# Dense expert stage: half of the PSUM sums leave through ScalarE, and gates lie in runs of 32 tokens

## The chip, the cores and the metric

The kernel runs on one core of one Trainium2 chip. The metric is device time in microseconds (us), the median of several runs; before the change it is 3537.24 us over 3 runs (3536.96 to 3545.42).

The core's engines are named as the profile names them: PE is TensorE's matmul stream and PEld its weight loads, DVE is VectorE, ACT is ScalarE, POOL is GpSimd, SP is SyncE. Each runs its own list of instructions in order. Matmuls write to PSUM, which has eight banks of 128 partitions by 512 float32.

## The reference

One decoder block over 1024 tokens of width 1024. First come RWKV-7 time mixing and differential attention, merged by gates. The change touches what follows, a feed-forward layer of 16384 single-vector experts. Each token picks 16 experts in each of 8 heads; an expert is a pair of keys (e1, e2), each one of 128:

```
ids   = e1 * 128 + e2                        # 8 x 16 experts per token
gates = softmax(vals)                        # per head
act   = gelu(sum_d u_tab[ids] * h) * gates   # 128 numbers per token
y     = sum_e act[e] * v_tab[ids[e]]
x     = x + y                                # then the final RMSNorm
```

## The kernel before

**Two ways through the experts.** For the first four blocks of 128 tokens, `peer` gathers the chosen rows of the tables: POOL issues an indirect DMA (L792) that brings one row of 1024 for each of 128 tokens into a tile `uv`, of which there are five. DVE forms the dot product with `hb` (L814) or adds the row, weighted, to `acc` (L821). That is 512 gathers from `u` and 512 from `v`. For the last four blocks (512 tokens) `dense` computes all 16384 experts and multiplies by a gate that is zero where the token did not choose the expert.

**The gates stage.** `gates` builds the dense gates, four tokens at a time. DVE makes one-hot tiles of the first key (`oh`, L833) and of the second (`ohb`, L837); ACT scales the second by the gate values (`ohg`, L842); PE multiplies the two for each token into a bank `gb` (L843): 128 second keys on the partitions by 128 first keys. ACT copies `gb` into `st` (L844), and every 32 tokens a DMA writes `st` to the scratch tensor `gd_s`, in groups of CE = 4 first keys. PE takes each float32 product as two MATMUL instructions, so 512 products are 1024 of them. Meanwhile `ahead` computes the first 16 values of `ua` below and keeps them in `a_s`.

**The dense stage.** `dense` loops over the 128 first keys e. `head(e)` loads two half tiles of `u` (`wraw`), splits each into a high and a low part (ACT `whi` L153, DVE `wlo` L154), multiplies them with the normalized tokens into a PSUM bank `ua`, takes GELU on ACT (`gw`, L883), multiplies by the gates on DVE (L884), and splits the product (ACT `ah` L175, DVE `al` L176) and two half tiles of `v` (`vh` L175, `vl` L176). The gates of four keys come in one tile `gt` of [512 tokens, 4 keys], so that L884 reads every fourth element of it.

The outputs are eight tiles (four token blocks by two halves of 512 columns). Six stay in PSUM banks `yk` through all 128 keys. The other two ("moved") have no bank of their own: for every second e, `rest` sums CV = 2 keys into a bank `yr`, and DVE adds that bank to `acc` in SBUF (L904), 128 times in all. `yr` and `ua` share the two banks of `zbank`.

**What sets the order.** The code is written as one program, and a tile scheduler places the instructions on each engine at build time, by its own costs. It sets the operations of `peer`, which come last in the program, between those of the gates stage and of the dense stage. From then on each engine's list is fixed.

Of the kernel before, what the change touches and what calls it, by code (L numbers as in the profile page):

```python
# [8 lines left out]
F32 = mybir.dt.float32  # L9
# [4 lines left out]
AF = mybir.ActivationFunctionType  # L14
OP = mybir.AluOpType
# [3 lines left out]
P = 128  # L19
# [17 lines left out]
NE = 16  # L37
# [2 lines left out]
CHO = (1, 1, 1, 1, 0)  # L40
CHB = CH * (CH + 1)
CE = 4
CV = 2
NV = (8, 6)

# [2 lines left out]
def body(ctx: ExitStack, tc: tile.TileContext, ins, out, dbg=None):  # L48
    nc = tc.nc
# [9 lines left out]
    def zbank(name):  # L59
        return ps.tile([P, 512], F32, name=name, tag="zb", bufs=2)  # L60
# [4 lines left out]
    def abank(name):  # L65
        return ps.tile([P, 512], F32, name=name, tag="ab", bufs=2)
# [10 lines left out]
    def at(name, dt=F32):  # L77
        return hp.tile([P, 512], dt, name=name, tag="at", bufs=NA)
# [4 lines left out]
    def t4(name):  # L83
        return hp.tile([P, D], F32, name=name, tag="t4", bufs=N4)
# [89 lines left out]
    def split(src, hi, lo):  # L174
        nc.scalar.activation(hi, src, AF.Copy)  # L175
        nc.vector.tensor_tensor(lo, src, hi.bitcast(F32), op=OP.subtract)  # L176

    def mm3(o, ah, al, bh, bl, first, last):
        nc.tensor.matmul(o, ah, bh, start=first, stop=False)  # L179
        nc.tensor.matmul(o, ah, bl, start=False, stop=False)  # L180
        nc.tensor.matmul(o, al, bh, start=False, stop=last)  # L181
# [614 lines left out]
    def finish(acc, rows, pool, tag, bufs):  # L796

        ssq = pool.tile([P, 1], F32, name="ssqf", bufs=2)
        fnw = pool.tile([P, D], F32, name="fnw", tag=tag, bufs=bufs)
        nc.scalar.activation(fnw, acc, AF.Square, accum_out=ssq)  # L800
        nc.sync.dma_start(fnw, ins["fnw"].to_broadcast([P, D]))
        r = invroot(ssq, 1, 1.0 / D, 1e-6, pool=pool)
        nc.vector.scalar_tensor_tensor(acc, acc, r[:, 0:1], fnw, op0=OP.mult, op1=OP.mult)
        nc.sync.dma_start(out[rows, :], acc)
# [19 lines left out]
    def gates(sp, a, sl, eye8):  # L824

        e1, g = sl[:, 0:P], sl[:, 2 * P:3 * P]
        e2 = sl[:, 3 * P:].bitcast(BF)[:, 0:P]
        nc.scalar.activation(e2, sl[:, P:2 * P], AF.Copy)
        for q in range(0, P, 32):
            st = sp.tile([P, P // CE, 32, CE], F32, name="st", bufs=2)  # L830
            for t in range(0, 32, 4):
                o1 = sp.tile([P, 4, P], F32, name="oh", bufs=4)
                nc.vector.tensor_tensor(o1, eye_row[:, None, :].to_broadcast([P, 4, P]),  # L833
                                        e1[:, q + t:q + t + 4, None].to_broadcast([P, 4, P]), op=OP.is_equal)
                if t % 8 == 0:
                    o2 = sp.tile([P, P, 8], BF, name="ohb", bufs=2)
                    nc.vector.tensor_tensor(o2, eye8, e2[:, None, q + t:q + t + 8].to_broadcast([P, P, 8]),  # L837
                                            op=OP.is_equal)
                b = abank("gb")
                o3 = sp.tile([P, 4, P], F32, name="ohg", bufs=2)  # L840
                for k in range(4):
                    nc.scalar.activation(o3[:, k], o2[:, :, t % 8 + k], AF.Copy, scale=g[:, q + t + k:q + t + k + 1])  # L842
                    nc.tensor.matmul(b[:, k * P:(k + 1) * P], o3[:, k], o1[:, k], start=True, stop=True)  # L843
                nc.scalar.activation(st[:, :, t:t + 4, :].rearrange("p c t f -> p t c f"),  # L844
                                     b.rearrange("p (t c f) -> p t c f", t=4, f=CE), AF.Copy)
            s0 = a * P + q
            nc.sync.dma_start(ins["gd_s"][:, :, s0:s0 + 32, :].rearrange("c p t f -> p c t f"), st)

    def dots(e, W, fh, fl):
        b = zbank("ua")[:, :W]  # L850
        wmul(b, ins["ut"][e], lambda k: fh[:, k, :W], lambda k: fl[:, k, :W], step=8)
        return b
# [8 lines left out]
    def dense(t0, W, fh, fl):  # L861

        TT = W // P
        fp = ctx.enter_context(tc.tile_pool(name="fp", bufs=1))
        acc = []
        for a in range(TT):
            acc.append(t4("accd"))
            nc.sync.dma_start(acc[a], ins["x1s"][t0 + a * P:t0 + (a + 1) * P, :])
        outs = [(a, 0) for a in range(TT)] + [(a, 1) for a in range(TT)][::-1]
        banks = (rbank, rbank, rbank, obank, abank, abank)  # L870
        kept = {o: f("yk") for o, f in zip(outs, banks)}
        moved = outs[len(banks):]
        gt = [None]

        def head(e):

            if e % CE == 0:
                gt[0] = fp.tile([P, 512, CE], F32, name="gt", bufs=2)
                nc.sync.dma_start(gt[0][:, :W], ins["gd_s"][e // CE, :, 0:W, :])
            w = fp.tile([P, 512], F32, name="gw", bufs=2)[:, :W]  # L880
            if e < NE:
                nc.sync.dma_start(w, ins["a_s"][e, :, 0:W])
            nc.scalar.activation(w, w if e < NE else dots(e, W, fh, fl), AF.Gelu)  # L883
            nc.vector.tensor_tensor(w, w, gt[0][:, :W, e % CE], op=OP.mult)  # L884
            v = []
            ah, al = at("ah", F32R)[:, :W], at("al", F32R)[:, :W]
            split(w, ah, al)
            for h, c in enumerate(HALVES):
                raw = fp.tile([P, 512], F32, name="vraw", bufs=NVR)
                nc.sync.dma_start(raw, ins["v"][e * P:(e + 1) * P, c])  # L890
                v.append([fp.tile([P, 512], F32R, name=n, tag=f"v{h}", bufs=NV[h]) for n in ("vh", "vl")])
                split(raw, *v[h])
            return ah, al, v

        def add(o, b, r, first, last):
            ts = slice(o[0] * P, (o[0] + 1) * P)
            mm3(b, r[0][:, ts], r[1][:, ts], *r[2][o[1]], first, last)

        def rest(o, rs):
            b = zbank("yr")  # L900
            for i, r in enumerate(rs):
                add(o, b, r, i == 0, i == CV - 1)
            y = acc[o[0]][:, HALVES[1]]
            nc.vector.tensor_tensor(y, y, b, op=OP.add)  # L904

        rs = [head(0)]
        for e in range(P):
            nxt = head(e + 1) if e + 1 < P else None
            full = rs[:CV] if e % CV == 0 and e else None
            if full:  # L910
                rs = rs[CV:]
            for n, (o, b) in enumerate(kept.items()):
                if full and n in MV:
                    rest(moved[MV.index(n)], full)
                add(o, b, rs[-1], e == 0, e == P - 1)
            rs.append(nxt)
        for o in moved:
            rest(o, rs[:CV])
        for a in range(TT):
            for h in range(2):  # L920
                if (a, h) in kept:
                    y = acc[a][:, HALVES[h]]
                    nc.vector.tensor_tensor(y, y, kept[a, h], op=OP.add)
            finish(acc[a], slice(t0 + a * P, t0 + (a + 1) * P), fp, "gt", 2)
# [13 lines left out]
    if "nopeer" not in dbg:  # L938
        with tc.tile_pool(name="sp", bufs=1) as sp:
            eye_f = sp.tile([P, P * 8], F32, name="eye_f", bufs=1)  # L940
            nc.sync.dma_start(eye_f, ins["eye8"])
            eye8 = sp.tile([P, P, 8], BF, name="eye8", bufs=1)
            nc.vector.tensor_copy(eye8.rearrange("p e t -> p (e t)"), eye_f)
            o = W - ND * P
            fh, fl = fh[:, :, o:W], fl[:, :, o:W]
            for a, c in enumerate(late[o // P:]):
                gates(sp, a, choose(*c), eye8)
                ahead(sp, ND * P, fh, fl, range(a * NE // ND, (a + 1) * NE // ND))
            todo += [(c[2], *choose(*c)) for c in late[:o // P]]
        dense(t0 + o, ND * P, fh, fl)  # L950
        for t in todo:
            peer(*t)


def prepare(inputs):
# [31 lines left out]
    for b in (16, 32):  # L987
# [17 lines left out]

SCRATCH = {"x1s": (T, D), "hfs": (T, D), "k_s": (4, P, T), "v_s": (4, P, T),
           "y_s": (4, 8, P, 512), "g_s": (4, 16, P, 512),
           "gd_s": (P // CE, P, 512, CE), "a_s": (NE, P, 512),
           "m_s": (2, 2, 8 * CHB), "z_s": (2, 2, 8 * CHB)}


# [16 lines left out]
```

## Time and profile before

| | us |
|---|---|
| median of 3 runs | 3537.24 |
| the profiled execution | 3524.41 |
| its span, first to last instruction | 3522.5 |
| PE / DVE / ACT / POOL busy | 3075.7 / 2923.6 / 1363.1 / 1332.3 |

The profile is of one execution, 0.4% below the median of the runs. Times count from the start of its span. The gates stage lies about 1637 to 1967, the dense stage (first to last L904) 2033 to 3483, and the end of `peer` and the final norms 3483 to 3523. A row of a group gives its busy time, the mean duration of one in ns, and the idle time of its engine just before them with what ended that time. Successive instructions of DVE overlap a little, so busy time is below count times mean.

### The profile page before, as it was taken

The numbers are of one execution on the slowest core, as the hardware profiler recorded it, in microseconds if no ns is written. First come the engines' busy times: TensorE is split into PE (matmuls) and PEld (weight loads), VectorE is DVE, ScalarE is ACT, GpSimd is POOL, SyncE is SP. The second block draws the span as 40 slices with busy tenths as digits, with TensorE's granted clock in tenths as the row PEclk, the third lists the DMA queues.
The fourth block names the chain that finished last, engine by engine and source line by source line (L and its number), as shares of the span: only waits on it lengthen the run. The fifth ranks groups of instructions, "written<-read, shape, count | busy, mean of one in ns | idle before, by whom it ended". The sixth has DMA issues, their size and how long they took to land. (4 is left out here: it accounts for less than half of the span.)

```text
span 3522.5 us, 50906 instructions
## 1 busy us (share of the span) xinstructions
PE 3075.7 (87%) x17382; PEld 2399.4 (68%) x17382; DVE 2923.6 (83%) x6546; ACT 1363.1 (39%) x2506; POOL 1332.3 (38%) x1036
## 2 busy tenths in 40 slices
PE   6999998998778966798888589999999999899994
PEld 5777776776556654676666467777777777777773
DVE  4656558978888878999877689998999999899998
ACT  3444434443424421336989433222223232222321
POOL 0000000025543454411223336655655655556554
PEclk9999999989788987899988799999999999999997
DMA  4222444257675789854678989999999999999997
GB/s 129 76 75 72 121 162 155 83 165 239 217 255 178 253 293 311 289 183 136 208 215 279 323 314 342 353 349 341 348 343 351 348 350 354 348 344 357 340 336 270
DMA packets 407524, 898.68 MB, mean 255 GB/s; under 512 B 69024, under 2 KB 140000, under 8 KB 403168
## 3 DMA queue, kind: packets, MB, share of 16 engines
q0 software_dynamic: 147456, 536.94, 43.7%
q1 hardware_dynamic: 259808, 358.49, 30.2%
q8 instruction: 137, 2.24, 0.3%
q14 instruction: 123, 1.01, 0.1%
HBM read 829.22 MB, written 66.07 MB: 254 GB/s over the span
## 5 line engine op out<-in xcount | busy, mean ns | idle before, releaser
L792 POOL DMA_INDIRECT uv<-u,ids x512 | 663.8, 1296 | 1259.3 <-DVE uv L814 622.4
L792 POOL DMA_INDIRECT uv<-v,ids x512 | 667.4, 1304 | 534.3 <-DVE acc L821 379.8
L821 DVE SCALAR_TENSOR_TENSOR acc<-uv,act,acc 128x1024 f32<-128x1024 f32 x512 | 655.5, 1280 | 63.8 <-DMA uv<-v,ids 57.2
L814 DVE SCALAR_TENSOR_TENSOR uv<-uv,hb 128x1024 f32<-128x1024 f32 x512 | 615.6, 1218 | 74.1 <-DMA uv<-u,ids 73.5
L153 ACT ACTIVATE whi<-wraw 128x512 fp32r<-128x512 f32 x552 | 344.2, 629 | 702.2 <-PE z L169 205.5
L168 PE MATMUL ua<-fh,whi 128*128 128x512 f32 x1024 | 427.8, 418 | 95.2 <-DVE accd L904 71.8
L154 DVE TENSOR_TENSOR wlo<-wraw,whi 128x512 fp32r<-128x512 f32 x552 | 373.3, 684 | 140.4 <-ACT whi L153 129.8
L169 PE MATMUL ua<-fl,whi 128*128 128x512 f32 x1024 | 421.5, 412 | 0.0
L175 ACT ACTIVATE ah<-gw 128x512 fp32r<-128x512 f32 x128 | 80.8, 631 | 657.2 <-DVE gw L884 657.2
L179 PE MATMUL yk<-vh,ah 128*128 128x512 f32 x768 | 305.3, 398 | 21.8 <-DMA gw<-a_s 18.1
L168 PEld LDWEIGHTS ua<-fh,whi 128*128 128x128 f32 x1024 | 203.6, 199 | 160.8 <-DVE accd L904 91.8
L180 PE MATMUL yk<-vl,ah 128*128 128x512 f32 x768 | 305.2, 397 | 7.6 <-DVE vl L176 7.5
L181 PE MATMUL yk<-vh,al 128*128 128x512 f32 x768 | 304.9, 397 | 1.3 <-DVE al L176 1.3
L168 PE MATMUL z<-hh,whi 128*128 128x512 f32 x672 | 275.5, 411 | 1.0 <-ACT whi L153 1.0
L172 PE MATMUL z<-hh,wlo 128*128 128x512 f32 x672 | 274.5, 409 | 0.6 <-DVE wlo L154 0.6
L169 PE MATMUL z<-hl,whi 128*128 128x512 f32 x672 | 274.6, 409 | 0.0
L172 PE MATMUL ua<-fh,wlo 128*128 128x512 f32 x1024 | 264.7, 399 | 6.2 <-DVE wlo L154 6.2
L843 PE MATMUL gb<-oh,ohg 128*128 128x128 f32 x1024 | 227.5, 343 | 42.4 <-ACT ohg L842 41.9
L843 PEld LDWEIGHTS gb<-oh,ohg 128*128 128x128 f32 x1024 | 167.0, 210 | 105.7 <-ACT ohg L842 69.3
L169 PEld LDWEIGHTS ua<-fl,whi 128*128 128x128 f32 x1024 | 203.8, 199 | 43.7
L842 ACT ACTIVATE ohg<-ohb,sl 128x128 f32<-128x128 bf16 x512 | 230.1, 551 | 1.9 <-DVE ohb L837 1.9
L172 PEld LDWEIGHTS ua<-fh,wlo 128*128 128x128 f32 x1024 | 195.0, 191 | 49.9 <-DVE wlo L154 7.1
(320 smaller groups left out, 5672.3 us busy)
## 6 DMA issues: line engine op xcount, KB each, us to landing
wraw<-ut SPq DMA_DIRECT2D x256, 256.0 KB, 6.3
vraw<-v SPq DMA_DIRECT2D x256, 256.0 KB, 6.6
wraw<-w_in SPq DMA_DIRECT2D x168, 256.0 KB, 2.8
gd_s<-st SPq DMA_DIRECT2D x16, 2048.0 KB, 12.4
gt<-gd_s SPq DMA_DIRECT2D x32, 1024.0 KB, 9.2
wraw<-wq SPq DMA_DIRECT2D x64, 256.0 KB, 2.8
g_s<-sgo SPq DMA_DIRECT2D x32, 256.0 KB, 2.7
wraw<-proj SPq DMA_DIRECT2D x32, 256.0 KB, 4.2
```

The costliest lines, as they stand in the source:

```text
L153: nc.scalar.activation(hi, raw, AF.Copy)
L154: nc.vector.tensor_tensor(lo, raw, hi.bitcast(F32), op=OP.subtract)
L168: nc.tensor.matmul(o, hi, xh(k), start=(k == 0), stop=False)
L169: nc.tensor.matmul(o, hi, xl(k), start=False, stop=False)
L172: nc.tensor.matmul(o, lo, xh(k), start=False, stop=(k == n - 1))
L179: nc.tensor.matmul(o, ah, bh, start=first, stop=False)
L180: nc.tensor.matmul(o, ah, bl, start=False, stop=False)
L181: nc.tensor.matmul(o, al, bh, start=False, stop=last)
L792: nc.gpsimd.indirect_dma_start(out=t, out_offset=None, in_=ins[src], in_offset=bass.IndirectOffsetOnAxis(ap=ids[:, j:j + 1], axis=0))
L814: nc.vector.scalar_tensor_tensor(u, u, 1.0, hb, op0=OP.mult, op1=OP.mult, accum_out=act[:, j:j + 1])
L821: nc.vector.scalar_tensor_tensor(acc, v, act[:, j:j + 1], acc, op0=OP.mult, op1=OP.add)
L843: nc.tensor.matmul(b[:, k * P:(k + 1) * P], o3[:, k], o1[:, k], start=True, stop=True)
```

## The change

Three edits. First, in `gates` the four products of a bank are interleaved: token k of four takes every fourth column from k on, so that ACT's copy writes, for each first key, four tokens that lie side by side. `st`, `gd_s` and `gt` then hold, for each first key, QT = 32 contiguous tokens. Second, L884 reads `gt` in runs of 32 contiguous elements. Third, `rest` copies `yr` to a new SBUF tile `ye` (two of them) by ACT, and DVE adds `ye`.

```
-            st = sp.tile([P, P // CE, 32, CE], F32, name="st", bufs=2)
+            st = sp.tile([P, P, QT], F32, name="st", bufs=2)
...
-                    nc.tensor.matmul(b[:, k * P:(k + 1) * P], o3[:, k], o1[:, k], start=True, stop=True)
-                nc.scalar.activation(st[:, :, t:t + 4, :].rearrange("p c t f -> p t c f"),
-                                     b.rearrange("p (t c f) -> p t c f", t=4, f=CE), AF.Copy)
-            s0 = a * P + q
-            nc.sync.dma_start(ins["gd_s"][:, :, s0:s0 + 32, :].rearrange("c p t f -> p c t f"), st)
+                    nc.tensor.matmul(b[:, k:512:4], o3[:, k], o1[:, k], start=True, stop=True)
+                nc.scalar.activation(st[:, :, t:t + 4], b.rearrange("p (e t) -> p e t", t=4), AF.Copy)
+            nc.sync.dma_start(ins["gd_s"][:, :, (a * P + q) // QT].rearrange("c p f t -> p c (f t)"),
+                              st.rearrange("p (c f) t -> p c (f t)", f=CE))
...
-                gt[0] = fp.tile([P, 512, CE], F32, name="gt", bufs=2)
-                nc.sync.dma_start(gt[0][:, :W], ins["gd_s"][e // CE, :, 0:W, :])
+                gt[0] = fp.tile([P, 512 // QT, CE, QT], F32, name="gt", bufs=2)
+                nc.sync.dma_start(gt[0][:, :W // QT], ins["gd_s"][e // CE, :, 0:W // QT])
...
-            nc.vector.tensor_tensor(w, w, gt[0][:, :W, e % CE], op=OP.mult)
+            w3 = w.rearrange("p (q t) -> p q t", t=QT)
+            nc.vector.tensor_tensor(w3, w3, gt[0][:, :W // QT, e % CE, :], op=OP.mult)
...
+            t = fp.tile([P, 512], F32, name="ye", bufs=2)
+            nc.scalar.activation(t, b, AF.Copy)
             y = acc[o[0]][:, HALVES[1]]
-            nc.vector.tensor_tensor(y, y, b, op=OP.add)
+            nc.vector.tensor_tensor(y, y, t, op=OP.add)
```

The lists of PE and POOL keep their order. Below the lists are given as they stand; line numbers after the change are larger by one to three (L884 becomes L885, L904 becomes L907, L175 becomes L176, L821 becomes L822).

ACT in the dense stage, the stretch of one key e in which `rest` runs, before and then after:

```order
L883 ACTIVATE gw<-ua 128x512
L175 ACTIVATE ah<-gw 128x512
L175 ACTIVATE vh<-vraw 128x512 x3
L153 ACTIVATE whi<-wraw 128x512 x2
L883 ACTIVATE gw<-ua 128x512
```

```order
L883 ACTIVATE gw<-ua 128x512
L905 ACTIVATE ye<-yr 128x512
L176 ACTIVATE ah<-gw 128x512
L176 ACTIVATE vh<-vraw 128x512
L905 ACTIVATE ye<-yr 128x512
L176 ACTIVATE vh<-vraw 128x512 x2
L154 ACTIVATE whi<-wraw 128x512 x2
L883 ACTIVATE gw<-ua 128x512
```

Where nothing stood between the split of `gw` and those of `v`, there are now two copies of `yr`: one ahead of `ah` (in some places behind it), and one ahead of the second and third `vh` and of `whi`.

DVE at the end of the dense stage, from the last `vl` on, before and then after:

```order
L176 TENSOR_TENSOR vl<-vraw,vh 128x512
L904 TENSOR_TENSOR accd<-accd,yr 128x512
L821 SCALAR_TENSOR_TENSOR acc<-uv,act,acc 128x1024
L923 TENSOR_TENSOR accd<-accd,yk 128x512 x4
L821 SCALAR_TENSOR_TENSOR acc<-uv,act,acc 128x1024
L923 TENSOR_TENSOR accd<-accd,yk 128x512 x2
L904 TENSOR_TENSOR accd<-accd,yr 128x512
L821 SCALAR_TENSOR_TENSOR acc<-uv,act,acc 128x1024
L904 TENSOR_TENSOR accd<-accd,yr 128x512
```

```order
L177 TENSOR_TENSOR vl<-vraw,vh 128x512
L907 TENSOR_TENSOR accd<-accd,ye 128x512
L822 SCALAR_TENSOR_TENSOR acc<-uv,act,acc 128x1024
L926 TENSOR_TENSOR accd<-accd,yk 128x512
L822 SCALAR_TENSOR_TENSOR acc<-uv,act,acc 128x1024
L926 TENSOR_TENSOR accd<-accd,yk 128x512 x5
L822 SCALAR_TENSOR_TENSOR acc<-uv,act,acc 128x1024
L907 TENSOR_TENSOR accd<-accd,ye 128x512 x2
```

Behind the last of these rows the list before still holds 13 operations on gathered rows (L821), and the list after 3 (L822). From the first L884 on there are 658 such operations (L814 and L821) in either list; ten of them have moved from behind the last L904 to places among the 128 keys.

## Rows read from the trace of the kernel before

**Rows 1.** Stages: busy time and count of each engine, granted clock, DMA share, GB/s

```profile
core 0: us, PE busy (x) PEld busy (x) DVE busy (x) ACT busy (x) POOL busy (x), PEclk, DMA share, GB/s
1637.00:1967.00 330.00, 279.34 (x1245) 206.60 (x1244) 270.56 (x642) 305.39 (x684) 80.52 (x67) 0.90 0.73 224
...
2033.00:3483.00 1450.00, 1362.41 (x5702) 1085.27 (x5700) 1346.57 (x1796) 417.92 (x723) 836.26 (x641) 0.98 0.95 343
3483.00:3523.00 40.00, 0.00 (x0) 0.00 (x0) 27.91 (x84) 5.64 (x10) 10.97 (x9) 0.50 0.73 256
```

**Rows 2.** Waits in the dense stage: us in total, times, longest us

```profile
ACT ah L175 <- DVE gw L884: 653.3, 118, 9.8
POOL uv L792 <- DVE acc L821: 264.1, 156, 7.2
...
PE ua L168 <- DVE accd L904: 71.8, 39, 5.4
...
DVE uv L814 <- DMA uv<-u,ids: 48.7, 63, 2.3
```

**Rows 3.** Waits of DVE alone in the dense stage, rest of the list

```profile
DVE acc L821 <- DMA uv<-v,ids: 32.4, 55, 2.2
DVE gw L884 <- ACT gw L883: 12.0, 7, 4.2
```

**Rows 4.** Groups of DVE's and ACT's instructions, 2000 to 3522

```profile
L154 DVE TENSOR_TENSOR wlo<-wraw,whi 128x512 fp32r<-128x512 f32 x221 | 147.3, 684 | 0.0
...
L884 DVE TENSOR_TENSOR gw<-gw,gt 128x512 f32<-128x512 f32 x128 | 138.1, 1079 | 13.0 <-ACT gw L883 13.0
...
L904 DVE TENSOR_TENSOR accd<-accd,yr 128x512 f32<-128x512 f32 x128 | 86.7, 678 | 0.0
...
L883 ACT ACTIVATE gw<-ua 128x512 f32<-128x512 f32 x112 | 67.0, 598 | 118.3 <-PE ua L172 118.2
```

**Rows 5.** One line: a product whose second operand has runs of 64 (L306)

```profile
L306 DVE TENSOR_TENSOR KR<-kk,Ep x8: 679/686/691, 93.9 to 1222.7; 128x512 f32<-128x512 f32 x8
```

**Rows 6.** Gathered tiles in the dense stage: count, ns min/median/max; issue to landing

```profile
L792 POOL DMA_INDIRECT uv<-v,ids x375: 932/1145/1947, 2075.9 to 3480.1; - x188
L821 DVE SCALAR_TENSOR_TENSOR acc<-uv,act,acc x371: 1266/1284/1331, 2092.8 to 3481.6; 128x1024 f32<-128x1024 f32 x186
L814 DVE SCALAR_TENSOR_TENSOR uv<-uv,hb x271: 1207/1218/1295, 2031.9 to 3227.9; 128x1024 f32<-128x1024 f32 x136
...
DMA to landing us min/median/max: 4.5/7.2/11.7
```

**Rows 7.** Stretches of 50 us with the highest DMA share, columns as rows 1

```profile
2483.00:2533.00 50.00, 47.15 (x192) 37.72 (x192) 45.90 (x77) 13.94 (x24) 30.23 (x24) 0.93 0.98 359
2633.00:2683.00 50.00, 44.74 (x182) 35.78 (x181) 45.69 (x70) 13.26 (x24) 26.93 (x22) 0.93 0.98 368
2933.00:2983.00 50.00, 48.52 (x207) 38.40 (x206) 46.91 (x79) 14.76 (x26) 27.69 (x22) 1.00 0.98 359
3183.00:3233.00 50.00, 44.81 (x186) 35.56 (x185) 47.81 (x79) 14.24 (x25) 31.76 (x24) 0.97 0.99 369
```

**Rows 8.** PE in the gates stage, in order of time: start, us

```profile
1722.69 1.54 PE L172 MATMUL ua<-fh,wlo 128*128 128x512 f32 x6
...
1725.27 1.59 PE L843 MATMUL gb<-oh,ohg 128*128 128x128 f32 x8
```

**Rows 9.** Group of the gate products, gates stage

```profile
L843 PE MATMUL gb<-oh,ohg 128*128 128x128 f32 x1024 | 227.5, 343 | 42.4 <-ACT ohg L842 41.9
```

**Rows 10.** ScalarE lines L842 and L828: 128 elements, strided and contiguous

```profile
L842 ACT ACTIVATE ohg<-ohb,sl x512: 502/523/682, 1643.5 to 1963.6; 128x128 f32<-128x128 bf16 x171
...
L828 ACT ACTIVATE sl<-sl x4: 300/302/310, 1642.0 to 1892.7; 128x128 bf16<-128x128 f32 x4
```

**Rows 11.** The last L904, and the last operation on a gathered row

```profile
3482.76 0.68 DVE L904 TENSOR_TENSOR accd<-accd,yr 128x512 f32<-128x512 f32 x1
...
3505.02 1.28 DVE L821 SCALAR_TENSOR_TENSOR acc<-uv,act,acc 128x1024 f32<-128x1024 f32 x1
```

More of the change, by code (lines that the diff above doesn't have):

```diff
@@ L42 @@
 CE = 4
+QT = 32
 CV = 2
@@ L828, in gates @@
         nc.scalar.activation(e2, sl[:, P:2 * P], AF.Copy)
-        for q in range(0, P, 32):
-            st = sp.tile([P, P // CE, 32, CE], F32, name="st", bufs=2)
-            for t in range(0, 32, 4):
+        for q in range(0, P, QT):
+            st = sp.tile([P, P, QT], F32, name="st", bufs=2)
+            for t in range(0, QT, 4):
                 o1 = sp.tile([P, 4, P], F32, name="oh", bufs=4)
@@ L1007 @@
            "y_s": (4, 8, P, 512), "g_s": (4, 16, P, 512),
-           "gd_s": (P // CE, P, 512, CE), "a_s": (NE, P, 512),
+           "gd_s": (P // CE, P, 512 // QT, CE, QT), "a_s": (NE, P, 512),
            "m_s": (2, 2, 8 * CHB), "z_s": (2, 2, 8 * CHB)}
```

## The prediction

> **What bounds the kernel now.** I read first where the three edits act, in the busy time by stages [rows 1], since the shares over the whole span are means over stages with different limits. One edit acts in the gates stage (1637 to 1967), the other two in the dense stage (2033 to 3483). In the dense stage three resources look full at once: PE is busy for 1362.4 of 1450 us, DVE for 1346.6, and the DMA engines for 0.95 of the time at 343 GB/s. ACT has 417.9 us of work there and POOL 836.3. So the second thing to read is who waits for whom. DVE waits for nothing that PE makes: its waits are for gathered rows, 48.7 us at L814 and 32.4 us at L821, and 12.0 us for ACT [rows 2, 3]. Its row L904 has no idle time before it [rows 4], so PE has always finished `yr` when DVE comes to it. The others wait for DVE: ACT 653.3 us for the product with the gates (L884), POOL 264.1 us for L821 to free a buffer, PE 71.8 us for L904 to free a bank [rows 2]. DVE, in its fixed order, is therefore what sets the pace of the dense stage; the gathers are close behind it, and PE has little room.
>
> In the gates stage ACT is busy for 305.4 of 330 us, and PE waits 41.9 us for its `ohg` [rows 1, 9]: ACT bounds it.
>
> **The change part by part.** Step 1, L884 with contiguous gates. The row has 128 instructions of 1079 ns [rows 4]. The same operation on two contiguous tiles takes 684 ns (L154) [rows 4], and with a second operand in runs of 64 it takes 686 ns (L306) [rows 5], so runs of 32 should cost nothing. That is 128 x (1079 - 684) = 50.6 us off DVE, in its own order, with ACT's `ah` waiting right behind it. Bounds: a run of 32 could cost twice the little that a run of 64 does, which leaves 50 us; at worst the product keeps its 1079 ns, and the saving is zero.
>
> Step 2, the add from SBUF. L904 reads a bank and takes 678 ns; with both operands in SBUF I take L154's 684 [rows 4]: 128 x 6 ns = +0.8 us. So moving the operand makes the add no shorter here.
>
> [...]
>
> Step 3, the copy of `yr`. ACT gains 128 instructions like L883, which reads a bank of the same size in 598 ns [rows 4]: 76.5 us. ACT goes from 417.9 to about 494 of 1450 us, so this lies beside other work. It is a new wait in ACT's order: behind a copy stand `ah`, or two `vh` and `whi`, for which DVE and then PE wait. I cost that at nothing: DVE comes to the first add after the product with the gates, and as a rule after `al` as well, so that PE has long finished `yr`, and ACT has hundreds of us of waiting to put the copy in. If the cover were gone, each add would wait for one ACT copy, 128 x 0.6 = 77 us; that is the upper bound. Below nothing: PE's 71.8 us of waiting for L904 go, since the bank is free about 0.6 us after PE fills it. I count no gain, because DVE does not wait for PE. PE's next wait is for DVE's splits.
>
> Step 4, the gate products. The 1024 PE instructions now write every fourth column. No row of before shows a strided PSUM write. Eight of these instructions take 1.59 us [rows 8], so a column leaves about every 1.59 / 8 / 128 = 1.55 ns; six of `ua` take 1.54 us with 512 columns each, one column every 0.50 ns. The write could be three times slower than a contiguous one before it showed, so I take zero. From above: strided reads did cost, L884's 1079 against 684, a factor of 1.58, and ACT's 523 against 302 ns [rows 10]. A factor of 1.58 on 199 ns is 1024 x 0.115 = 118 us, of which PE's idle time in the stage, 330 - 279.3 = 50.7 us, takes up part: 67 us later. No mechanism gives a gain here. ACT's copy into `st` writes runs of four elements before and after, and the DMAs keep size and destination.
>
> [...]
>
> Step 5, ten gathered operations moved from the end into the dense stage. DVE's work from 2033 to the end stays the same: ten of about 1.2 us more before the last add, ten fewer behind it. I therefore make the sum over both stretches.
>
> Step 6, what is late next. DVE's work from 2033 to the end of the span (3522.5) is 1346.6 + 27.9 = 1374.5 us [rows 1], and its idle time 1489.5 - 1374.5 = 115. With 50 us less work the gathers have to come faster. Five buffers go round: POOL's instruction (1.15), the way to landing (7.2) and the operation itself (1.28) are 9.6 us, 1.9 us for each of five [rows 6]; 371 + 271 = 642 operations in 1450 us are one every 2.26 us. So the present pace has some room, but landings of up to 11.7 us already make DVE wait. From one side the extra waits are zero or a little below, since shorter stretches without L821 make smoother demand. From the other, the gathers keep their pace and take back all 50 us. Which is nearer: the four stretches of 50 us in which the DMA engines were busiest, 0.98 to 0.99 at 359 to 369 GB/s [rows 7], have DVE busy for 45.90, 45.69, 46.91 and 47.81, mean 46.6, against a mean of 1346.6 / 29 = 46.4 over the dense stage. More traffic than the change needs (343 x 1450 / 1415 = 351 GB/s) came without more waiting. I take 15 us, on the side of these rows.
>
> Sum: -50.6 + 0.8 + 15 = -34.8 us. The profiled execution took 3524.4 us, its span and 1.9 around it; 3489.6 after it, a factor of 0.990. On the median shown, 3537.2, that is 3502 us.
>
> **Rivals.** (a) The strided write slows the gate products. For it: both strided reads in SBUF are slow. Against it: these products hand over columns at a third of the rate of `ua`. Place: L843, in the gates stage. With the factor above the stage ends 67 us later, net +32, 3569 us. It decides the sign once the stage grows by more than 35 us, that is when an instruction takes (50.7 + 35) / 1024 = 0.084 us more than its 0.199.
>
> (b) The gathers set the pace. For it: 0.95 DMA share, and DVE's 81.1 us of waits on them. Against it: the busiest stretches [rows 7], and POOL's waits for DVE. The dense stage then keeps its length, and only the end, where DVE runs on from the last L904 at 3482.76 to the last L821 at 3505.02 [rows 11], gets shorter, some 0 to 10 us: 3527 to 3537.
>
> (c) ACT's order delays the splits: a copy that waits for PE holds up `vh` and `whi`. For it: ACT's list is fixed. Against it: L904 had no idle time before it. At 77 us of waits less the 35 gained it is +42, 3579 us.
>
> (d) The gates' layout does not shorten L884, because something other than the stride makes it slow. Against it: L306. Time as before, 3537 us.
>
> (e) The whole saving and more: gathers no later, PE freed of its 71.8 us, DVE's idle time shorter by some 15. That is -65 us, 3472.
>
> **How the numbers follow.** A difference of 0.3%, 10.6 us, is about what a measurement of this kernel can tell from none. The forecast, 3475 to 3523 around 3502, has a chance of 0.66; (a) 0.10, (b) 0.13, (c) 0.04, (d) 0.03, (e) 0.04. Faster than 3526.6: the forecast and (e), 0.70. Within 0.3%: (b) and (d), 0.16. Slower: (a) and (c), 0.14. The range goes from 3470, just below (e), to 3540, above (b) and (d); it leaves out the two slower rivals and a little below.
>
> **What would show it.** L885 near 684 ns, and `ye` copies near 600 ns on ACT. No wait of PE for the add of `yr`. L907 without idle time before it; if it has some, with ACT as its releaser, step 3 was wrong. PE's gate products at 1.6 us for eight and the gates stage still 330 us long; if not, step 4. DVE's waits for gathers in the dense stage 80 to 100 us; if they are at 130, the pace was the gathers' and step 6 was wrong. The end from the last add to the end of the span about half of its 40 us. A time above 3527 would make the prediction wrong.

## The result and the profile after

The changed kernel takes 3514.4 us (median of 6 runs, 3502.6 to 3524.1) against 3540.4 of the kernel before in the same comparison: ratio 0.9927, 95% interval 0.9907 to 0.9946, that is 26 us or 0.7% faster. The forecast was 35 us.

The two profiled executions differ less, 3524.4 and 3514.0 us. The stretch up to the gates stage, whose instructions stand in the same order in both kernels, took 1640 us before and 1656 after; in the later runs it lay between 1633 and 1666. So I compare from the gates stage on. From the first one-hot tile to the first add of `yr` it is 393.3 us before and 388.0 after, from there to the last such add 1449.1 and 1446.0, and from there to the end 39.7 and 22.1. The first of these three stretches tells nothing of the change: in the later runs it took 387.8 to 389.3 us with the gates as before and 387.4 to 392.1 with the new ones.

The stages of the kernel after (start and end, length, busy time of PE, PEld, DVE, ACT and POOL, then clock, DMA share, GB/s); the second row begins with the first add and answers to the dense row of [rows 1]:

```profile
1655.00:1979.00 324.00, 275.45 (x1229) 204.27 (x1228) 267.01 (x629) 304.04 (x682) 80.17 (x66) 0.89 0.73 226
...
2044.10:3490.80 1446.70, 1363.65 (x5705) 1082.92 (x5703) 1311.99 (x1805) 467.33 (x850) 851.31 (x650) 0.98 0.95 347
3490.80:3512.20 21.40, 0.00 (x0) 0.00 (x0) 15.74 (x73) 5.63 (x10) 0.00 (x0) 0.50 0.67 245
```

DVE has 34 us less work in the dense stage, although ten more gathered operations lie in it, and yet the stage is only 3 us shorter. What became of the rest stands in the waits there (us in total, times, longest):

```profile
ACT ah L176 <- DVE gw L885: 720.4, 112, 11.6
...
DVE uv L815 <- DMA uv<-u,ids: 63.1, 72, 3.5
DVE acc L822 <- DMA uv<-v,ids: 48.2, 71, 2.1
...
PE ua L169 <- ACT ye L905: 39.9, 12, 5.9
...
ACT ye L905 <- PE yr L182: 30.6, 32, 7.3
```

DVE's waits for gathered rows rose from 81.1 us [rows 2, 3] to 111.3. The groups that answer to [rows 4]:

```profile
L155 DVE TENSOR_TENSOR wlo<-wraw,whi 128x512 fp32r<-128x512 f32 x225 | 150.9, 688 | 9.8 <-ACT whi L154 9.6 <-PE ua L173 0.2
L885 DVE TENSOR_TENSOR gw<-gw,gt 128x512 f32<-128x512 f32 x128 | 88.4, 691 | 17.0 <-ACT gw L883 17.0
L907 DVE TENSOR_TENSOR accd<-accd,ye 128x512 f32<-128x512 f32 x128 | 87.8, 686 | 0.0
```

The product with the gates (L885) fell from 1079 to 691 ns; the add (L907) went from 678 to 686.

### The profile page after: what moved, and what is told of

Read it like the earlier page. It is cut to its first block, busy times and chain, and to the rows that moved or that the text cites. A ratio compares the mean times of both kernels' runs of the same rounds, so it can differ in the third digit from the quotient of the medians.

```text
span 3512.2 us, 51039 instructions
## 1 busy us (share of the span) xinstructions
PE 3085.0 (88%) x17382; PEld 2404.1 (68%) x17382; DVE 2876.8 (82%) x6546; ACT 1412.5 (40%) x2634; POOL 1334.3 (38%) x1036
## 5 line engine op out<-in xcount | busy, mean ns | idle before, releaser
L793 POOL DMA_INDIRECT uv<-u,ids x512 | 655.2, 1280 | 1255.3 <-DVE uv L815 626.6
L793 POOL DMA_INDIRECT uv<-v,ids x512 | 677.9, 1324 | 519.2 <-DVE acc L822 372.4
L822 DVE SCALAR_TENSOR_TENSOR acc<-uv,act,acc 128x1024 f32<-128x1024 f32 x512 | 655.4, 1280 | 72.2 <-DMA uv<-v,ids 65.7
L169 PE MATMUL ua<-fh,whi 128*128 128x512 f32 x1024 | 419.7, 410 | 61.5 <-ACT ye L905 39.9
L176 ACT ACTIVATE ah<-gw 128x512 fp32r<-128x512 f32 x128 | 80.8, 632 | 727.0 <-DVE gw L885 723.1
L844 PE MATMUL gb<-oh,ohg 128*128 128x128 f32 x1024 | 228.3, 344 | 40.3 <-ACT ohg L843 37.8
```

The source lines that it names most:

```text
L169: nc.tensor.matmul(o, hi, xh(k), start=(k == 0), stop=False)
L793: nc.gpsimd.indirect_dma_start(out=t, out_offset=None, in_=ins[src], in_offset=bass.IndirectOffsetOnAxis(ap=ids[:, j:j + 1], axis=0))
L822: nc.vector.scalar_tensor_tensor(acc, v, act[:, j:j + 1], acc, op0=OP.mult, op1=OP.add)
L844: nc.tensor.matmul(b[:, k:512:4], o3[:, k], o1[:, k], start=True, stop=True)
```

## The experiments

All ratios are to the kernel before on the same chip. The columns in us are from one profiled execution each: from the first add of `yr` to the last, from there to the end, and DVE's waits for gathered rows between the two adds. The runs come from several chips: the kernel before took 3516.6 us on that of e1 to e4, 3543.0 on that of e5 to e8, 3513.3 on that of f1 and f2. So the ratios are the safer comparison between these groups. NVR is the number of tiles into which `v` is loaded ahead, 6 where nothing is said.

| kernel | buffers | ratio (95%) | dense | end | waits |
|---|---|---|---|---|---|
| before | 5 | 1 | 1449.1 | 39.7 | 81.1 |
| whole change | 5 | 0.9927 (0.9907 to 0.9946) | 1446.0 | 22.1 | 111.3 |
| e1 layout only | 5 | 0.9934 (0.9916 to 0.9953) | 1433.6 | 39.8 | 104.8 |
| e2 copy only | 5 | 0.9963 (0.9951 to 0.9976) | 1463.1 | 21.5 | 87.6 |
| e4 before | 6 | 0.9857 (0.9839 to 0.9875) | 1406.4 | 37.6 | 42.8 |
| e3 layout only | 6 | 0.9770 (0.9754 to 0.9785) | 1377.8 | 37.7 | 51.8 |
| f2 layout only, again | 6 | 0.9772 (0.9749 to 0.9795) | 1373.9 | 37.4 | 49.0 |
| e6 layout only, NVR 4 | 6 | 0.9811 (0.9786 to 0.9836) | 1394.7 | 37.8 | 45.2 |
| e5 whole, NVR 4 | 6 | 0.9805 (0.9781 to 0.9830) | 1396.5 | 22.3 | 36.3 |
| f1 whole, NVR 5, one `ye` | 6 | 0.9763 (0.9740 to 0.9785) | 1376.2 | 20.9 | 38.7 |
| e7 layout only, NVR 4 | 7 | 0.9771 (0.9747 to 0.9796) | 1381.2 | 33.7 | 20.0 |
| e8 whole, half of v | 5 | 0.9862 (0.9832 to 0.9891) | 1417.6 | 21.6 | 82.5 |

**e1 and e2: the two halves of the change.** e1 takes the copy out of the changed kernel, e2 puts it alone into the kernel before (the lines are shortened).

```
# e1, against the changed kernel             # e2, against the kernel before
-  t = fp.tile([P, 512], F32, name="ye"...)  +  t = fp.tile([P, 512], F32, name="ye"...)
-  nc.scalar.activation(t, b, AF.Copy)       +  nc.scalar.activation(t, b, AF.Copy)
-  nc.vector.tensor_tensor(y, y, t, ...)     -  nc.vector.tensor_tensor(y, y, b, ...)
+  nc.vector.tensor_tensor(y, y, b, ...)     +  nc.vector.tensor_tensor(y, y, t, ...)
```

Expected of e1:

> The change without the copy of yr: gates in runs of 32 tokens, VectorE adds yr from PSUM as before; every engine's list is that of before. Theory (VectorE's own order sets the pace of the dense stage, and the gathers behind it take back part of what it saves): the product with the gates at 685 ns, VectorE's work 50 us less, its waits for gathered rows 80 to 110 us in place of 81, ratio to before 0.991 to 0.995, about 3515 us, as the whole change. Rival 1 (the copy costs, since PE waits for it and it sits in ScalarE's order): this is faster than the whole change, below 0.989. Rival 2 (the gain is in the end of the kernel, from the ten gathered operations that the scheduler moved ahead, and these come with the copy): no gain here, 0.997 to 1.002, with the 39 us between the last add and the end as before.

Measured: 3494.6 us against 3516.6, 0.9934, as the theory had it. The dense stage and the end of e1, and its waits:

```profile
2023.50:3457.80 1434.30, 1354.49 (x5702) 1081.42 (x5700) 1300.92 (x1795) 417.80 (x724) 816.57 (x642) 0.98 0.95 347
3457.80:3496.90 39.10, 0.00 (x0) 0.00 (x0) 27.42 (x83) 5.61 (x10) 10.58 (x9) 0.50 0.74 256
```

```profile
DVE uv L815 <- DMA uv<-u,ids: 55.1, 71, 2.3
DVE acc L822 <- DMA uv<-v,ids: 49.7, 75, 1.9
...
PE ua L169 <- DVE accd L905: 64.3, 36, 4.2
```

With every list as before, only the duration of one group was changed: DVE loses 45.5 us of work (1346.4 to 1300.9) and the dense stage 15.5; the 39 us at the end stay. DVE's waits for gathers took 23.7 us back. PE still waits 64.3 us for the add, and that did not keep the gain away. Rivals 1 and 2 fell.

Expected of e2:

> The copy of yr alone, gates as before (product with the gates at 1079 ns). The lists of all engines are those of the whole change, with the ten gathered operations moved ahead of the last add. Theory: VectorE's work is unchanged, so time is within 0.3% of before, ratio 0.998 to 1.002; PE's 72 us of waits for the add shrink to about 40 (waits for the copy) and buy nothing. Rival 1 (the copy costs): 1.003 to 1.010. Rival 2 (the end carries the gain): 0.993 to 0.996.

Measured: 3503.7 us, 0.9963. That is 13 us faster, a little less than rival 2 had it, and clearly more than the theory, which was wrong here. The same two stretches of e2:

```profile
2027.20:3491.00 1463.80, 1368.19 (x5699) 1083.46 (x5697) 1357.86 (x1805) 467.02 (x850) 883.79 (x650) 0.98 0.95 343
3491.00:3511.80 20.80, 0.00 (x0) 0.00 (x0) 15.64 (x73) 5.64 (x10) 0.00 (x0) 0.54 0.71 252
```

The dense stage is 14.0 us longer with the ten moved operations, the end 18.2 shorter. In the trace that leaves 4 us; how the rest of the 13 came about one profile does not tell (the execution profiled took 3513.5 us, 10 above the median of e2). The lists of DVE, ACT and POOL are those of the whole change in e2 and those of the kernel before in e1, so the move of the ten comes with the copy and not with the layout. The two gains do not add up: 22 us for the layout and 13 for the copy, each by itself, and 26 for both. Beside the layout the copy's worth can't be told from nothing: the intervals of e1 and of the whole change overlap for the most part.

**e3 and e4: a sixth buffer for gathered rows.** The theory for the lost half of the gain was that five buffers limit how closely gathers follow DVE. The rival was the rate of the DMA engines.

```
+    more = [None, 0]
+
     def gather(src, ids, j):
-        t = pp_.tile([P, D], F32, name="uv", bufs=NU)
+        more[1] += 1
+        if more[0] and more[1] % (NU + 1) == 0:
+            t = more[0].tile([P, D], F32, name="uv6", bufs=1)
+        else:
+            t = pp_.tile([P, D], F32, name="uv", bufs=NU)
...
+        if bi >= 1 and not more[0]:
+            more[0] = ctx.enter_context(tc.tile_pool(name="xp", bufs=1))
```

> e1 with a sixth buffer for gathered rows in the dense stage (from the second block's rows of v on). Theory (five buffers and about 7 us from issue to landing limit how fast gathers follow VectorE): waits for gathered rows fall to 40 to 70 us, 25 to 45 us faster than e1, ratio to before 0.980 to 0.986. Rival (the DMA engines' rate limits the gathers, 0.95 busy at 347 GB/s): one more buffer only lengthens the way to landing from 7.2 to some 8.5 us, waits as in e1, time within 6 us of e1.

> The kernel before with the same sixth buffer. Theory (buffers limit the gathers): waits for gathered rows fall from 81 to 30 to 50 us, ratio 0.988 to 0.993. Rival (DMA rate): 0.998 to 1.002 with longer landings. Together with e3: if buffers are the limit, the layout is worth more with six of them (e3 against e4, 40 to 50 us) than with five (e1 against before).

Measured: e4 0.9857, 48 us faster than before with no other edit; e3 0.9770, 57 us faster than e1 on the same chip. The waits fell as the theory had it, and both gains are larger than it had them. The stage and DVE's waits in e3:

```profile
2025.20:3403.70 1378.50, 1343.86 (x5706) 1080.56 (x5704) 1299.77 (x1795) 427.65 (x723) 812.07 (x642) 0.99 0.97 361
```

```profile
DVE uv L821 <- DMA uv<-u,ids: 42.8, 51, 3.4
DVE gw L893 <- ACT gw L891: 17.0, 9, 5.6
DVE acc L830 <- DMA uv<-v,ids: 9.0, 15, 1.7
```

and in e4:

```profile
2022.80:3429.90 1407.10, 1350.85 (x5702) 1081.12 (x5700) 1343.78 (x1795) 420.41 (x723) 841.01 (x642) 0.98 0.96 354
```

```profile
DVE uv L820 <- DMA uv<-u,ids: 37.7, 47, 4.6
DVE gw L892 <- ACT gw L891: 12.4, 7, 4.0
DVE acc L829 <- DMA uv<-v,ids: 5.1, 7, 1.9
```

The DMA engines moved 361 GB/s in e3 where they moved 343 before, and a gather's median from issue to landing was 7.4 to 7.6 us against 7.2 to 7.3. So their rate was no ceiling at 343 or 347.

Besides the buffer the lists of e4 and e3 differ a little from before: the scheduler issues one gather of `v` ahead of many of `u`, and in DVE's list up to four gathered operations stand earlier, between about 2357 and 2626 us of e4. That stretch became 10.4 us shorter; in the rest of the dense stage DVE's list is that of the kernel before, and e4 gained 32.3 us there. So the new order does not carry the gain.

The layout alone is worth 31.3 us with six buffers (3468.6 to 3437.3) against 22.0 with five (3516.6 to 3494.6), each known to about 6 us either way. In the profiles, from the first add to the end, it saved 28.5 and 15.4 us, of some 44 and 45 us of DVE's work (totals over both stretches): with six buffers two thirds of the saved work became time, with five one third. By the medians it is seven tenths and a half. I had expected 40 to 50 us between e3 and e4; what is missing in the profiles are 9 us more of waits for gathers, 5 for the GELU, and 2 elsewhere. PE is 97% busy in e3: the bounds lie close together.

**e5, e6 and e7: copy and layout with more buffers.** To make room, NVR went from 6 to 4 in all three. e7 has two more buffers in place of one; the last four lines below are its own, against e3's edit.

```
-NVR = 6
+NVR = 4
...
-        if more[0] and more[1] % (NU + 1) == 0:
-            t = more[0].tile([P, D], F32, name="uv6", bufs=1)
+        if more[0] and more[1] % (NU + 2) < 2:
+            t = more[0].tile([P, D], F32, name="uv6", bufs=2)
```

> The whole change with a sixth buffer for gathered rows; NVR is 4 in place of 6, to make room (two fewer tiles of v loaded ahead). Against e6, which is the same without the copy of yr. Theory A (what the copy gives with five buffers, 0.996, comes from the ten gathered operations that its list has ahead of the last add, where the end is bound by gathers): 3 to 12 us faster than e6, ratio to before 0.973 to 0.980, the end from the last add 20 to 24 us long in place of 37. Theory B (with six buffers PE is the nearest bound, 97% busy in e3, and its 22 us of waits for the add count): about 15 us faster than e6, with PE's waits for the bank gone. Rival (the copy sits behind the split of gw in ScalarE's order and PE waits for it up to 6 us at a time): slower than e6 by 0 to 15 us.

> e3 with NVR 4 in place of 6: control for e5 and e7. Theory: v is loaded early enough with four tiles, ratio 0.976 to 0.980, as e3 (0.977). Rival: ScalarE's split of v waits for the load, 0.982 to 0.990.

> e6 with a seventh buffer for gathered rows. Theory (with six buffers the gathers are no longer the nearest bound; VectorE and PE are, at 94 and 97% busy, and the DMA engines at 0.97 and 361 GB/s): 5 to 15 us faster than e6, waits for gathered rows 52 to about 35 us, those left lying in the stretches of u. Rival (buffers still limit): 30 us or more faster.

e6, 0.9811, is 4 thousandths behind e3, between its theory and its rival. DVE now waits 29.8 us for ACT's split of `v` (0.4 us in e3), and ACT waits 78.7 us over the whole execution for loads of `v` (at most 17.4 in e3). DVE's waits in e6, in e5, which is the same with the copy, and in e7, in this order:

```profile
DVE uv L821 <- DMA uv<-u,ids: 39.3, 48, 3.4
DVE vl L177 <- ACT vh L176: 29.8, 23, 4.2
```

```profile
DVE vl L177 <- ACT vh L176: 35.8, 24, 4.3
DVE uv L821 <- DMA uv<-u,ids: 33.5, 43, 4.3
DVE gw L893 <- ACT gw L891: 4.6, 4, 3.0
DVE acc L830 <- DMA uv<-v,ids: 2.8, 3, 1.5
```

```profile
DVE vl L177 <- ACT vh L176: 42.2, 28, 7.1
DVE uv L821 <- DMA uv<-u,ids: 20.0, 24, 3.1
```

e5 has an end of 22 us in place of 38, and from the first add to the end of the span it is 14 us shorter than e6; but its median is that of e6 (3474.8 and 3474.85), and in its profile the unchanged stretch ahead of the gates took 1666 us against 1651. The medians show neither the gain of theory A nor that of theory B nor the rival's loss, so whether the copy gains anything with six buffers stays open between e5 and e6. PE's waits at the bank did not go, as theory B had it: 15.7 us for the copy, where e6 has 39.2 for the add. e7 gained 13 us on e6 in the medians, as the theory said, with intervals of the ratios that just overlap; of the waits for gathers 20.0 us were left, and waits for the split of `v`, 42.2 us, took part of their place; its loads come late, ACT waits 95.1 us for them over the whole execution.

**e8: fewer bytes.** The changed kernel with the second half tile of `v` not loaded; the first half's tile is split in its place, so half of the dense part's output columns come from other numbers.

```
-                raw = fp.tile([P, 512], F32, name="vraw", bufs=NVR)
-                nc.sync.dma_start(raw, ins["v"][e * P:(e + 1) * P, c])
+                if h == 0:
+                    raw = fp.tile([P, 512], F32, name="vraw", bufs=NVR)
+                    nc.sync.dma_start(raw, ins["v"][e * P:(e + 1) * P, c])
```

> The whole change, five buffers, with the second half tile of v not loaded: its products use the first half's data, so half of the output columns of the dense part are computed from other numbers. 128 loads of 256 KB less, 33 of about 502 MB in the stage, while the instructions of the compute engines stay. Theory (the time of one gather and five buffers limit, and that time depends on how busy the DMA engines are): landing falls from 7.2 to 6.5 to 6.9 us, the waits for gathered rows from 111 to 70 to 90 us, time 15 to 35 us less than the whole change, ratio 0.983 to 0.989. Rival (the DMA engines' rate alone limits, six buffers only kept them busier): the stage shortens in proportion to the bytes, 6.5% or some 90 us, ratio 0.968 or less.

Measured: 0.9862, waits 41.4 and 41.1 us for rows of v and u. 33.5 MB less, 6.7% of the stage's bytes, made the stage 28 us or 2% shorter than that of the whole change. So with less traffic DVE waits less for rows (82.5 us in place of 111.3), but the stage doesn't follow the bytes: the rival fell. That the way to landing got shorter, as the theory has it, is not shown; the trace of e8 does not tell it. The six tiles of `v` also reach twice as far ahead here; DVE waited only 1.2 us for the split of `v` in the changed kernel, so little can have come of that.

**f1 and f2: a faster version.** f1 is the whole change with six buffers, NVR 5 and one `ye`; f2 repeats e3 beside it.

```
-NVR = 6
+NVR = 5
-            t = fp.tile([P, 512], F32, name="ye", bufs=2)
+            t = fp.tile([P, 512], F32, name="ye", bufs=1)
```

> The whole change with a sixth buffer for gathered rows; one tile ye in place of two and NVR 5 in place of 6, to make room. Against f2, on the same chip. Theory (with six buffers the copy's list still shortens the end by 15 us, as in e5 against e6, and lengthens the dense part by about 10 for the ten operations it takes in; NVR 5 costs a third or half of the 17 us that NVR 4 cost from the first add on): ratio to before 0.974 to 0.979, within 6 us of f2 on either side. Rival (with one ye the copy waits for VectorE's add, PE for the copy): 10 to 25 us slower than f2.

> e3 once more, to compare with f1 and to see what a second set of runs gives. Theory: ratio to before 0.975 to 0.980 (e3 had 0.977). Rival (e3's gain was its chip's): 0.983 or more.

f1 took 3427.1 us, 0.9763, f2 3434.9, 0.9772, before 3513.3. The rival, 10 to 25 us slower, fell. The intervals of the two overlap, so the copy's worth is not settled here either; both are far ahead of the change as it was made (0.9927). The dense stage and the end of f1:

```profile
2022.10:3399.00 1376.90, 1341.86 (x5705) 1077.92 (x5703) 1310.81 (x1806) 485.68 (x852) 832.13 (x649) 0.99 0.98 365
3399.00:3419.20 20.20, 0.00 (x0) 0.00 (x0) 14.78 (x72) 5.63 (x10) 0.00 (x0) 0.50 0.73 260
```

The DMA engines are at 0.98, PE at 97% and DVE at 95% of the stage. With the work as it stands, room for more than a few per cent is left in none of them.

## Why the prediction was right, and where it missed

**Step 1, right.** 128 x (1079 - 691) = 49.7 us against 50.6. The stride was the cause: with the layout alone the product takes 693 ns (e1), with the copy alone 1081 (e2). Rival (d) fell.

**Step 2, right.** The add from SBUF takes 686 ns where 684 were taken.

**Step 3, right as to the cost, wrong in a reason.** ACT does 128 copies in 75 us beside its other work, and DVE's add has 0.0 us of idle time before it:

```profile
L905 ACT ACTIVATE ye<-yr 128x512 f32<-128x512 f32 x128 | 75.0, 586 | 30.7 <-PE yr L182 30.6
```

But the bank is not always "free about 0.6 us after PE fills it". Where the copy stands behind `ah`, it waits for DVE's product with the gates. One such place in order of time, PE first, then ACT:

```profile
2628.65 0.40 PE L182 MATMUL yr<-vh,al 128*128 128x512 f32 x1
...
2637.06 0.80 PE L169 MATMUL ua<-fh,whi 128*128 128x512 f32 x1 [5.92 <-ACT ye L905]
```

```profile
2635.89 0.63 ACT L176 ACTIVATE ah<-gw 128x512 fp32r<-128x512 f32 x1 [9.24 <-DVE gw L885]
2636.43 0.58 ACT L905 ACTIVATE ye<-yr 128x512 f32<-128x512 f32 x1
```

`yr` was done at 2629.05, and its copy began at 2636.43, when `ah` had been released. So PE's waits at the bank fell only from 71.8 to 39.9 us. Of the twelve waits that are left, 36.7 us are ten such places, and in the other two the copy stands behind another instruction of ACT that waited for DVE: PE still waits for DVE, now by way of ACT. PE was also slower behind the wait: right behind these 5.92 us without work the granted clock is 0.50 from 2637.0 to 2640.5, and then 0.99 from 2640.7 to 2644.0; the first eight products took 3.6 us, the next eight 1.9.

Rival (c) was right that ACT's list holds something up, but not in what. ACT does wait 30.6 us for PE ahead of copies, yet DVE waited only 1.2 us for the split of `v` behind them. And "I count no gain" did not hold for the copy by itself: e2 is 13 us faster than before. Where these come from stays open, and beside the layout they do not show.

**Step 4, right.** The strided write costs nothing here. The group of products and eight of them in a row, after:

```profile
L844 PE MATMUL gb<-oh,ohg 128*128 128x128 f32 x1024 | 228.3, 344 | 40.3 <-ACT ohg L843 37.8 <-issue 2.1
```

```profile
1741.37 1.59 PE L844 MATMUL gb<-oh,ohg 128*128 128x128 f32 x8
```

344 ns against 343 [rows 9], 1.59 us against 1.59 [rows 8]. Rival (a) fell. These products hand over a column every 1.55 ns; faster ones were not tried.

**Step 5, right.** The end went from 39.7 to 22.1 us, and the dense stage took the ten operations in. e1 and e2 show that they move with the copy. That DVE's work over both stretches stays the same by this move holds too: 1373.8 us before, 1373.5 in e2.

**Step 6, the step that was mis-sized.** From the first add to the end of the span DVE's work fell from 1373.8 to 1327.7 us, by 46.1 where 49.8 were forecast, and its idle time rose from 115.0 to 140.4, by 25.4 where 15 were taken (31.3 more in the dense stage, 5.9 less at the end). The sum is -20.7 us in this pair of profiles, against -34.8; 26 us in the medians. The wait that grew is that for gathered rows, by 30 us to 111.3, between the forecast's 80 to 100 and the 130 that would have meant rival (b). Rival (b)'s mechanism is therefore half of the truth: in the profiles it took back more than half of the saving, and e3 and e4 show what it hangs on, the number of buffers.

What misled was the row chosen to decide between the two bounds, that the busiest 50 us stretches had DVE no less busy [rows 7]. It shows that the DMA engines could carry more (359 to 369 GB/s there against 343 over the stage), which e3 confirmed with 361 over its whole stage. But how busy DVE is does not tell how long it waits for rows, and that came out the other way: in these four stretches of the kernel before it waited for gathered rows 4.1, 4.7, 2.1 and 2.4 us, 3.3 on average, and in 50 us of the whole stage 2.8. "Without more waiting" was not so.

The number that bears on the buffers stood beside it: by the medians a round takes 9.6 us, and five buffers at the pace of before allow 5 x 2.26 = 11.3, at the pace hoped for 5 x 1415 / 642 = 11.0. That leaves 1.7 and 1.4 us of slack, while a gather's landing varies from 4.5 to 11.7 us [rows 6]. That the loss of a few tenths of slack is what was paid in waits is an estimate from these numbers; what e3 and e4 show is that one more buffer takes about half of the waits away (104.8 to 51.8 us and 81.1 to 42.8).

## What to carry to other kernels

Before an engine's saved work is counted as time, work out the round of the buffers that feed it, and its slack against the spread of one transfer's time: where the spread is the larger, expect part of the saving back as waits (here 25 us of 46, with an estimated slack of 1.4 us against landings of 4.5 to 11.7), and try one more buffer first. Read the waits themselves in the rows that are to decide, and not the busy time in their place. A buffer count can be worth more than the instruction that looks dear: here 48 us against 22. And a copy put in to free a resource early frees it only when the engine that copies gets there (at the place shown, 7.4 us after PE was done): look at what stands ahead of it in that engine's list.

## What the runs showed of the hardware beyond that

The 128 x 512 float32 product on VectorE took 1079 ns with one operand at a stride of 16 bytes (L884, before) and 691 with runs of 128 bytes (L885, after). The float32 gate products of 128 columns wrote to PSUM at a stride of 16 bytes in the time that they took without it (344 ns after, 343 before). The DMA engines moved 365 GB/s at 0.98 of their time in f1.
